# A list-scheduled transformer kernel: order of FFN product groups, a reordered attention step, and another split of the down projection

## The chip, the cores and the metric

The kernel runs on one core of one Trainium2 chip. The metric is the device time of one execution in microseconds (us). A core has a matrix engine (TensorE, PE in the rows; its weight loads are PEld), VectorE (DVE), ScalarE (ACT), GpSimd (POOL) and SyncE (SP), which here issues all DMAs. Each engine works through its own list of instructions in order.

## The reference

All arrays are float32, the width is 1024, the sequence is 1024 tokens. Two layers stand one behind the other, each a mixer and a feed-forward network (FFN) of hidden width 2816, and then a second block.

```
h = layer_norm(x * alpha + mixer(x))              # even: conv + linear recurrence; odd: attention
h = layer_norm(h * alpha + (silu(h @ w_gate) * (h @ w_up)) @ w_down)

# diff attention of 8 heads, two maps of 64 each, causal by chunks of 64
scores = einsum('bhmqd,bhmkd->bhmqk', q, k); p = softmax(where(mask, scores, NEG))
attn = p[:, :, 0] - lam * p[:, :, 1];  o = rms_norm(attn @ v) * (1 - lambda_init);  return o @ w_out

# second block: modulation by ada(cond), mLSTM + Fourier mixing, then relu(h @ w_ff1 + b)**2 @ w_ff2, width 4096
```

## The kernel before, in words

Every large matrix product runs as three matmuls with split operands (`mm3`, L235 to L237: high by high, low by high, high by low). A weight is loaded into a tile `raw`; `split` (L213, L214) makes the high part with a cast on ACT (`wh`, `wd`, `ht`) and the low part with a subtraction on DVE (`wl`, and again `wd`, `ht`). The order in which instructions stand on each engine comes from a list scheduler that takes ready work by program order, so moving a call in the code moves instructions on all engines; the engines then run the lists in order. Waits between engines are by semaphores.

The up and gate product of an FFN, and the first product of the second block's FFN (FF2 below), uses a scheme of seven products for a 2 x 2 block product. `product` issues them: `corner` (B11, into `wx`, copied to `keep`), T2 (`wy`, copied to `u2`), T1 (`wz`, copied to `p5`), T3 on top of `wy`, `corner2` (B21 on `wx`), B22 and T4. One term is 12 matmuls of 128 x 512. The sums of input rows that the scheme needs are made by `xn.sums` (L144 to L155) and `prepare` (L661 on, with L674 to L677 on the weights). Before the first `product`, `start()` issues six corner products, called fronts here (`EARLY` = 1, 1, 2, 2), from within the last stage of the mixer ahead, where `pipe` calls `more`; each front needs one weight's `wh` and `wl`.

The result of the up and gate products goes to DRAM (`hd`), and the down projection reads it back by `tokens` as tiles `ht`. It runs in parts over the hidden width: `PARTS1` for the two FFNs (8, 6, 4, 4 blocks of 128), `PARTS2` for FF2; for each part it walks over 8 tiles of 128 tokens (`down_tile`, matmuls `dn`, added to `xr` on DVE at L898). The letter of a part says in which pool its weights lie. The last part runs in a pipe with the first stages of what follows (norm, transposes, V weights, `pv` and `pi` matmuls). `weights(j)` loads and splits part j. In FF2 the down weights are scaled on DVE by a row `mrow` that a DMA brings (L1248, L1828), and a bias row is added to `xr` on GpSimd. The pool `rp` of `raw` tiles has three buffers. Beside FFN1 the modulation (`ada`) runs as side work: 48 loads of 512 KB, two steps of it at each down tile (`SDN` = 2).

Attention (`mixer_odd`) walks over 64 steps (head, tile of 128 queries). A step issues: `scores` of the step two further on (matmuls `sc`, L1049 and L1050; then on DVE a memset and the maximum at L1058 or L1063, on ACT exp at L1065, on DVE L1069 to L1072), some fills (12 matmuls each, `pq`, `pv` or `pw`, projections of the next head or of the output), `trans` (transposes `pt`, L1083, copied to `at` by ACT, L1085), more fills, and `pv` (matmuls `po`, L1098; then ACT L1102, GpSimd, DVE L1105 and L1106). `sc` has two PSUM buffers of 1024 columns; from tile 4 on a step takes both.

Of the kernel before, what the change touches and what calls it, by code (L numbers as in the profile page):

```python
# [11 lines left out]
F32R = mybir.dt.float32r  # L12
# [15 lines left out]
NF2 = 4096 // P  # L28
NEG = -1.0e30
EARLY, WAHEAD = (1, 1, 2, 2), 2  # L30
PARTS1 = ((8, "x"), (6, "u"), (4, "x"), (4, "u"))
PARTS2 = ((8, "x"), (6, "u"), (8, "x"), (6, "u"), (4, "x"))
L2 = 2
DV = 1
# [29 lines left out]
ME, MO = (0, 1, 2), (1, 0, 2)  # L64
# [96 lines left out]
class Net:  # L161
# [248 lines left out]
    def mixer_even(self, xr, xn, start):  # L410
# [220 lines left out]
        for c in range(NC1, 4):  # L631
            conv(c, 1)
        more = lambda i: start() if i == NTT - 1 else None
        self.pipe(pre + [(0, lambda i: feat(i - 4)), (LE, prod_a), (LE + ME[0], more), (LE + ME[1], more),
                         (LE + ME[2], more), (LE + 1, norm), (LE + 2, feat), (LE + 3, xn.sums), (LE + 3, more)],
                  range(4, 8))

    def mixer_end(self, xr, xn, layer):
# [61 lines left out]
    def product(self, o, x, keep, finish, sum22, early):  # L700

        nc = self.nc
        if not early:
            px = self.corner(o, x, keep)
        py = self.pa("wy")
        self.term(py, o["S2"], x, "T2", True, True)
        nc.vector.tensor_add(py, py, keep)
        u2 = self.tmp("u2")
        nc.scalar.copy(u2, py)
        pz = self.pa("wz")  # L710
        self.term(pz, o["S1"], x, "T1", True, True)
        p5 = self.tmp("p5")
        nc.scalar.copy(p5, pz)
        nc.vector.tensor_add(pz, pz, u2)
        self.term(py, o["S3"], x, "T3", False, True)
        sum22(py, p5)
        if not early:
            self.corner2(o, x, px, finish)
        self.term(pz, o["S4"], x, "B22", False, True)
        finish(0, 1, pz)  # L720
        self.term(py, o["A22"], x, "T4", False, True)
        finish(1, 0, py)

    def run_ffn(self, nf, x, src, nm, done, parts, down_weight, load, add, stages, side=None, add_half=None):
# [20 lines left out]
        def finisher(q, m):  # L745
            def finish(i, h, p):
                f, d = 2 * q + i, dst(q, i, h)
                done(m, f, d, p)
                if m == nm - 1:
                    j = part_of(f)  # L750
                    nc.sync.dma_start(hd[j][f - edges[j], :, half(h)], d)

            def sum22(py, p5):
                if m == 0:
                    c = dst(q, 1, 1)
                else:
                    c = p5
                nc.vector.tensor_add(c, py, p5)
                finish(1, 1, c)

            return finish, sum22
# [4 lines left out]
        def finish_first():  # L766
            o, p, (q, m), finish = begun.pop(0)
            self.corner2(o, x, p, finish)
# [19 lines left out]
        def prep(n):  # L788
            q, m = order[n]
            return self.prepare(src(2 * q, m), src(2 * q + 1, m), first=(q, m) not in started)  # L790

        o = prep(0)
        while begun:
            finish_first()
        for n, (q, m) in enumerate(order):
            nxt = prep(n + 1) if n + 1 < len(order) else None
            finish, sum22 = finisher(q, m)
            self.product(o, x, keep(q, m), finish, sum22, (q, m) in started)
            if m == nm - 1:
                ctx.pop(q)  # L800
            if n % 2:
                kept.pop(n // 2)
            o = nxt
            steps(SD[n % 2])

        def weights(j):
            n, kind = parts[j]
            ws = []
# [9 lines left out]
                ws.append((t[:, e, :], t[:, e + 1, :]))  # L818
            return ws

        def tokens(j, i):
            n, hs = parts[j][0], []
            for a in range(0, n, 4):
                e = min(n, a + 4)
                shape = (P, 2, e - a, P)
                if add_half is None and j == len(parts) - 1:
                    t = self.u("ht", shape, F32R)
                else:
                    t = self.wp.tile(list(shape), F32R, tag="w", name=self.name("ht"))
                raw = t[:, 1].bitcast(F32)  # L830
                nc.sync.dma_start(raw, hd[j][a:e, :, blk(i)].rearrange("f p t -> p f t"))
                self.split(t[:, 0], t[:, 1], raw)
                hs += [(t[:, 0, b, :], t[:, 1, b, :]) for b in range(e - a)]
            return hs

        todo = [(j, i) for j in range(len(parts)) for i in range(NTT)]
        ws, hs = {0: weights(0)}, {}

        def ahead(n):
            if n < len(todo) and todo[n] not in hs:  # L840
# [136 lines left out]
    def mixer_odd(self, x, xr, xn, start):  # L977
# [190 lines left out]
        for n, (hd, i) in enumerate(steps):  # L1168
            if i == 0:
                if hd < 7:  # L1170
                    for _ in fill:
                        pass

                def filler(hd=hd):
                    if hd < 7:
                        yield from qk(hd + 1)
                    if hd < 6:
                        yield from vals(hd // 2 + 1, hd % 2)
                    else:
                        for _ in last:  # L1180
                            yield

                fill = filler()
                left = list(shares[hd])
            if n + LEAD < len(steps):
                if steps[n + LEAD][1] == 0:
                    assert sum(left[:i]) >= 16
                scores(*steps[n + LEAD])
            k = left[i]
            for _ in range((k + 1) // 2):  # L1190
                next(fill, None)
            trans(hd, i)
            for _ in range(k // 2):
                next(fill, None)
            pv(hd, i)
        for _ in last:
# [3 lines left out]
        more = lambda i: start() if i == NTT - 1 else None  # L1200
        sums = lambda i: xn.sums(i) if i >= 4 else None
        self.pipe([(0, lambda i: heads4(i, 4)), (LO + MO[0], more), (LO + 2, feat), (LO + 1, norm), (LO, o_prod),
                   (LO + MO[1], more), (LO + MO[2], more), (LO + 3, sums), (LO + 3, more)])

    def ada(self):
        nc, A = self.nc, self.A
# [119 lines left out]
    def block2_mix(self, x, xr, xn, start):  # L1326
# [480 lines left out]
        def more(i):  # L1807
            if i == NTT - 1:
# [1 line left out]

        stats = lambda i: self.ln_stats(xr[i])
        self.pipe([(3, stats), (4, stats), (1, prep), (3, norm1), (4, norm2), (2, prod)] + [(m, more) for m in MF]
                  + [(LM, feat), (0, moments), (LM + 1, lambda i: xn.sums(i) if i >= 4 else None), (LM + 1, more)])

    def block2_ff(self, x, xr, out):
        nc, A = self.nc, self.A
        st = {}
        cnt = [0] * NTT

        def done(m, f, d, p):  # L1820
            nc.scalar.activation(d, p, AF.Relu, bias=self.c("b_ff1", f))
            nc.vector.tensor_mul(d, d, d)

        def down_weight(f):
            if f == 0:
                st["g2"] = self.mod_row(5)
            r = self.raw(A["w_f2"][f])
            nc.vector.tensor_mul(r, r, st["g2"])  # L1828
            return r

        def load(i):
            if i == 0:
                st["b2"] = self.u("b2")
                r12 = ROWS.index("b_ff2")
                nc.sync.dma_start(st["b2"], A["rows"][r12:r12 + 1, :].to_broadcast([P, D]))
                nc.gpsimd.tensor_mul(st["b2"], st["b2"], st["g2"])
            xr.append(self.u("xr"))
            nc.sync.dma_start(xr[i], self.xs[2][blk(i), :])

        def add(i, p, first, last):  # L1840
            nc.vector.scalar_tensor_tensor(xr[i], xr[i], ALPHA2 if first else 1.0, p, op0=ALU.mult, op1=ALU.add,
                                           accum_out=self.sum_of(xr[i]) if last and S4 else None)
            if cnt[i] == 1:
                nc.gpsimd.tensor_add(xr[i], xr[i], st["b2"])
            cnt[i] += 1

        def add_half(i, p, cs):
            nc.vector.tensor_add(xr[i][:, cs], xr[i][:, cs], p)

        def parts(i):  # L1850
            return [half(0), half(1)] if i in HN else [slice(0, D)]

        def norm_a(i):
            if i == 0:
                st["gb"] = self.gb("ln2_g", "ln2_b")
            self.ln_stats(xr[i])
            t, g = xr[i], st["gb"][0]
            mu, _, sign = self.moments[id(t)]
            for c in parts(i):
                nc.vector.scalar_tensor_tensor(t[:, c], t[:, c], mu, g[:, c], op0=ALU.subtract if sign > 0 else ALU.add,  # L1860
                                               op1=ALU.mult)

        def norm_b(i):
            t, b = xr[i], st["gb"][1]
            rs = self.moments.pop(id(t))[1]
            for c in parts(i):
                nc.vector.scalar_tensor_tensor(t[:, c], t[:, c], rs, b[:, c], op0=ALU.mult, op1=ALU.add)
                nc.sync.dma_start(out[blk(i), c], t[:, c])

        return self.run_ffn(NF2, x, lambda f, m: A["w_f1"][f], 1, done, PARTS2, down_weight, load, add,  # L1870
                            [(FT, norm_b), (1, norm_a)], add_half=add_half)

# [152 lines left out]
```

## Time and profile before

| | |
|---|---|
| median of 3 runs | 3423.69 us (3421.68 to 3425.16) |
| the profiled execution: its own time | 3421.3 us |
| its span, first to last instruction | 3419.5 us |
| mean granted TensorE clock | 0.985 of full |
| busy: PE, DVE, ACT, POOL | 3269.5, 2185.5, 1412.9, 265.6 us |

PE is busy for 96% of the span, so what the order of the lists can change is the rest, and the stretches in which PE is busy at a lower clock. In the rows below a wait is put down to the last releaser that the profile shows.

### The profile page before, as it was taken

The numbers are of one execution on the slowest core, as the hardware profiler recorded it, in microseconds if no ns is written. First come the engines' busy times: TensorE is split into PE (matmuls) and PEld (weight loads), VectorE is DVE, ScalarE is ACT, GpSimd is POOL, SyncE is SP. The second block draws the span as 40 slices with busy tenths as digits, with TensorE's granted clock in tenths as the row PEclk, the third lists the DMA queues.
The fourth block names the chain that finished last, engine by engine and source line by source line (L and its number), as shares of the span: only waits on it lengthen the run. The fifth ranks groups of instructions, "written<-read, shape, count | busy, mean of one in ns | idle before, by whom it ended". The sixth has DMA issues, their size and how long they took to land.

```text
span 3419.5 us, 40944 instructions
## 1 busy us (share of the span) xinstructions
PE 3269.5 (96%) x15588; PEld 2692.5 (79%) x15588; DVE 2185.5 (64%) x3445; ACT 1412.9 (41%) x2422; POOL 265.6 (8%) x458
## 2 busy tenths in 40 slices
PE   8998999999999999989999999999999989999998
PEld 7776788878877878877788878778777878878887
DVE  8997755555357677676765558654446876566635
ACT  4455433332237667655533332224334554432211
POOL 1011000000020111101000000013001300000201
PEclk9999999999999999999999999999999999999999
DMA  3131322235312111141332238721123333344312
GB/s 126 42 112 62 101 91 74 91 128 169 106 62 71 36 50 50 43 149 56 109 107 99 93 120 290 237 74 47 59 84 106 116 117 117 116 161 165 113 51 79
DMA packets 191764, 348.68 MB, mean 102 GB/s; under 512 B 14384, under 2 KB 105936, under 8 KB 191568
## 3 DMA queue, kind: packets, MB, share of 16 engines
q1 hardware_dynamic: 191568, 346.07, 30.6%
q8 instruction: 122, 2.00, 0.2%
q14 instruction: 74, 0.61, 0.1%
HBM read 268.41 MB, written 72.36 MB: 100 GB/s over the span
## 4 chain that ended last, share of the span: by engine, by line
PE 66%; DVE 13%; ACT 9%; DMA 5%; issue 4%; POOL 3%; SPq 0%; POOLq 0%; DVEq 0%; ACTq 0%
PE dn L236 6%; PE dn L235 6%; PE dn L237 6%; PE wy L235 4%; PE wy L236 4%; PE wy L237 4%; PE wx L235 3%; PE wx L237 3%; PE wx L236 3%; PE pi L235 3%; PE pi L236 3%; PE pi L237 2%; PE wz L235 2%; PE wz L237 2%; PE wz L236 2%
## 5 line engine op out<-in xcount | busy, mean ns | idle before, releaser
L213 ACT CAST wh<-raw 128x1024 fp32r<-128x1024 f32 (+1 forms) x275 | 282.7, 1048 | 405.1 <-DVE raw L677 138.1
L214 DVE TENSOR_TENSOR wl<-raw,wh 128x1024 fp32r<-128x1024 f32 (+1 forms) x275 | 334.3, 1233 | 132.1 <-ACT wh L213 128.1
L213 ACT CAST ht<-ht 128x512 fp32r<-128x512 f32 (+1 forms) x168 | 97.2, 580 | 448.0 <-DMA ht<-hd 438.7
L235 PE MATMUL dn<-wd,ht 128*128 128x512 f32 x704 | 274.4, 391 | 3.3 <-ACT wd L213 3.3
L236 PE MATMUL dn<-wd,ht 128*128 128x512 f32 x704 | 274.8, 390 | 1.3 <-DVE wd L214 1.2
L237 PE MATMUL dn<-wd,ht 128*128 128x512 f32 x704 | 274.4, 390 | 0.0
L235 PE MATMUL dn<-wh,ht 128*128 128x512 f32 x512 | 200.9, 392 | 10.8 <-DVE xr L898 6.7
L214 DVE TENSOR_TENSOR ht<-ht 128x512 fp32r<-128x512 f32 (+1 forms) x168 | 112.3, 673 | 153.2 <-ACT ht L213 152.4
L235 PE MATMUL wx<-bh,wh 128*128 128x512 f32 x480 | 192.2, 400 | 10.6 <-ACT keep L693 4.2
L237 PE MATMUL wx<-bh,wl 128*128 128x512 f32 x480 | 190.2, 397 | 11.2 <-DVE wl L214 11.2
L237 PE MATMUL dn<-wh,ht 128*128 128x512 f32 x512 | 200.3, 391 | 0.4 <-DVE ht L214 0.4
L236 PE MATMUL dn<-wl,ht 128*128 128x512 f32 x512 | 200.2, 391 | 0.0
L236 PE MATMUL wx<-bl,wh 128*128 128x512 f32 x480 | 190.3, 396 | 0.0
L235 PE MATMUL pi<-xh,wh 128*128 128x512 f32 x416 | 168.8, 406 | 7.8 <-DVE xl L214 7.8
L486 DVE SCALAR_TENSOR_TENSOR co<-ga,col,co 128x512 f32<-128x512 f32 (+18 forms) x240 | 165.4, 737 | 0.5
L237 PE MATMUL pi<-xh,wl 128*128 128x512 f32 x416 | 165.0, 397 | 0.0
L236 PE MATMUL pi<-xl,wh 128*128 128x512 f32 x416 | 164.9, 396 | 0.0
L235 PEld LDWEIGHTS dn<-wd,ht 128*128 128x128 f32 x704 | 132.3, 188 | 32.0 <-ACT wd L213 4.6
L236 PEld LDWEIGHTS dn<-wd,ht 128*128 128x128 f32 x704 | 132.4, 188 | 30.3 <-DVE wd L214 2.9
L237 PEld LDWEIGHTS dn<-wd,ht 128*128 128x128 f32 x704 | 132.4, 188 | 27.5
L287 POOL TENSOR_SCALAR nm<-sum 128x1 f32<-128x1 f32 x47 | 15.1, 322 | 1562.8 <-DVE xr L898 1323.1
L898 DVE SCALAR_TENSOR_TENSOR xr<-xr,dn 128x1024 f32<-128x1024 f32 x64 | 77.8, 1216 | 85.5 <-PE dn L237 81.3
(458 smaller groups left out, 8446.4 us busy)
## 6 DMA issues: line engine op xcount, KB each, us to landing
raw<-w_gu SPq DMA_DIRECT2D x100, 512.0 KB
hd<-g SPq DMA_DIRECT2D x152, 256.0 KB
raw<-w_f SPq DMA_DIRECT2D x70, 512.0 KB
ht<-hd SPq DMA_DIRECT2D x136, 256.0 KB
raw<-w_ada SPq DMA_DIRECT2D x48, 512.0 KB
raw<-w_dn SPq DMA_DIRECT2D x44, 512.0 KB
raw<-w_in SPq DMA_DIRECT2D x26, 512.0 KB
raw<-w_out SPq DMA_DIRECT2D x24, 512.0 KB
```

Of the source, the lines that this page charges most:

```text
L213: self.nc.scalar.copy(hi, src)
L214: (self.nc.gpsimd if pool else self.nc.vector).tensor_sub(lo, src, hi.bitcast(F32))
L235: mm(out, l[0], r[0], start=first, stop=False, **kw)
L236: mm(out, l[0], r[1], start=False, stop=False, **kw)
L237: mm(out, l[1], r[0], start=False, stop=last, **kw)
L287: (nc.vector if NMV else nc.gpsimd).tensor_scalar(nm, a, -1.0 / D, None, op0=ALU.mult)
L486: nc.vector.scalar_tensor_tensor(co[c][:, a:hi_], ga[c][:, a - s:hi_ - s], self.c("conv_w", 31 * c + 30 - s), co[c][:, a:hi_], op0=ALU.mul ...
L898: nc.vector.scalar_tensor_tensor(xr[i], xr[i], DN_ALPHA if first else 1.0, p, op0=ALU.mult, op1=ALU.add, accum_out=self.sum_of(xr[i]) if l ...
```

## The change

Six edits are made.

- `PARTS1` becomes 8, 4, 4, 6 blocks, and the `ht` tiles of the last part come from the `raw` pool of three buffers and no longer from another pool.
- In `product`, `corner2` (the 12 matmuls of B21) stands ahead of T3 and no longer behind it.
- `weights(0)`, the first part's down weights, is issued ahead of the last `product` and no longer behind it.
- In three stage pipes the last `more` (fronts five and six) stands ahead of `xn.sums` and no longer behind it.
- An attention step issues first fills, `trans`, `scores` of two steps on, second fills, `pv`.
- In FF2 a multiplication and eight additions of the bias row go from GpSimd to DVE.

```
-PARTS1 = ((8, "x"), (6, "u"), (4, "x"), (4, "u"))
+PARTS1 = ((8, "x"), (4, "u"), (4, "x"), (6, "u"))
...
-                         (LE + ME[2], more), (LE + 1, norm), (LE + 2, feat), (LE + 3, xn.sums), (LE + 3, more)],
+                         (LE + ME[2], more), (LE + 1, norm), (LE + 2, feat), (LE + 3, more), (LE + 3, xn.sums)],
...
         nc.vector.tensor_add(pz, pz, u2)
+        if not early:
+            self.corner2(o, x, px, finish)
         self.term(py, o["S3"], x, "T3", False, True)
         sum22(py, p5)
-        if not early:
-            self.corner2(o, x, px, finish)
         self.term(pz, o["S4"], x, "B22", False, True)
...
             finish, sum22 = finisher(q, m)
+            if nxt is None:
+                ws[0] = weights(0)
             self.product(o, x, keep(q, m), finish, sum22, (q, m) in started)
...
-        ws, hs = {0: weights(0)}, {}
+        hs = {}
...
                 if add_half is None and j == len(parts) - 1:
-                    t = self.u("ht", shape, F32R)
+                    t = self.rp.tile(list(shape), F32R, tag="raw", name=self.name("ht"))
...
+            k = left[i]
+            for _ in range((k + 1) // 2):
+                next(fill, None)
+            trans(hd, i)
             if n + LEAD < len(steps):
                 if steps[n + LEAD][1] == 0:
                     assert sum(left[:i]) >= 16
                 scores(*steps[n + LEAD])
-            k = left[i]
-            for _ in range((k + 1) // 2):
-                next(fill, None)
-            trans(hd, i)
             for _ in range(k // 2):
                 next(fill, None)
             pv(hd, i)
...
-                nc.gpsimd.tensor_mul(st["b2"], st["b2"], st["g2"])
+                nc.vector.tensor_mul(st["b2"], st["b2"], st["g2"])
...
-                nc.gpsimd.tensor_add(xr[i], xr[i], st["b2"])
+                nc.vector.tensor_add(xr[i], xr[i], st["b2"])
```

Three places show how the lists move. The first is DVE's list ahead of FFN0's first product, before; the weight's low part of the last front is `wl_2714`, the sums of the last tiles are `ts_2660` and `ts_2661`, their splits `bl` and `bs`, and `w_390_2755` belongs to the first product.

```order
L151 TENSOR_TENSOR ts_2660<-f_2631,ts_2660 128x512
L152 TENSOR_TENSOR ts_2661<-f_2631 128x512
L153 TENSOR_TENSOR ts_2661<-f_2229,ts_2660 128x512
L887 TENSOR_TENSOR g_2619<-g_2619,wx_2593 128x512
L214 TENSOR_TENSOR bl_2448<-ts_2660,bh_2447 128x8x128
L214 TENSOR_TENSOR bs_2453<-ts_2661,bs_2451 128x2x128
L214 TENSOR_TENSOR bs_2454<-ts_2661,bs_2452 128x2x128
L214 TENSOR_TENSOR bs_2461<-ts_2661,bs_2459 128x2x128
L214 TENSOR_TENSOR bs_2462<-ts_2661,bs_2460 128x2x128
L214 TENSOR_TENSOR wl_2714<-raw_2711,wh_2713 128x1024
L214 TENSOR_TENSOR w_390_2755<-raw_2753,w_390_2755 128x512
```

The same place on DVE in the changed kernel, where the last front's low part is `wl_2698` and the last tiles' sums are `ts_2729` and `ts_2730`.

```order
L214 TENSOR_TENSOR wl_2698<-raw_2695,wh_2697 128x1024
L214 TENSOR_TENSOR bs_2352<-f_2631,bs_2350 128x2x128
L214 TENSOR_TENSOR bs_2353<-f_2631,bs_2351 128x2x128
L153 TENSOR_TENSOR ts_2645<-f_2154,ts_2644 128x512
L214 TENSOR_TENSOR bl_2448<-ts_2644,bh_2447 128x8x128
L214 TENSOR_TENSOR bs_2453<-ts_2645,bs_2451 128x2x128
L214 TENSOR_TENSOR bs_2454<-ts_2645,bs_2452 128x2x128
L214 TENSOR_TENSOR bs_2461<-ts_2645,bs_2459 128x2x128
L214 TENSOR_TENSOR bs_2462<-ts_2645,bs_2460 128x2x128
L890 TENSOR_TENSOR g_2619<-g_2619,wx_2593 128x512
L214 TENSOR_TENSOR w_390_2755<-raw_2753,w_390_2755 128x512
L674 TENSOR_TENSOR raw_2753<-raw_2753 128x512
```

The low part now stands ahead of both groups of sums, and the first product's weight work stands ahead of the last group.

The second place is PE's list in attention at the start of a step, before; the matmuls `pv` are fills.

```order
L237 MATMUL pv_8054<-wh_7912,xl_6695 128x256
L1098 MATMUL po_8092<-v_6832,at_8072 128x128 x4
L1098 MATMUL po_8092<-v_6833,at_8078 128x128 x3
L1049 MATMUL sc_8109<-kh_7555,sq_7553 128x256
L1050 MATMUL sc_8109<-kl_7557,sq_7553 128x256
L1049 MATMUL sc_8109<-kh_7556,sq_7554 128x256
L1050 MATMUL sc_8109<-kl_7558,sq_7554 128x256
L235 MATMUL pv_8127<-wh_7906,xh_6694 128x256
```

In the changed kernel PE's list around the scores of such a step reads so.

```order
L237 MATMUL pv_8036<-wh_7906,xl_6619 128x256
L1086 MATMUL pt_8049<-ident,e_7865 128x128 x4
L1086 MATMUL pt_8056<-ident,e_7865 128x128 x3
L1052 MATMUL sc_8063<-kh_7537,sq_7535 128x128
L1053 MATMUL sc_8063<-kl_7539,sq_7535 128x128
L1052 MATMUL sc_8063<-kh_7538,sq_7536 128x128
L1053 MATMUL sc_8063<-kl_7540,sq_7536 128x128
L235 MATMUL pv_8036<-wh_7912,xh_6618 128x256
```

The scores stood right behind `po` of the step before, and now stand behind the first fills and the transposes of their own step.

The third place is SP's list of DMAs at the end of FF2's products, before; `hd_18281` is written with the products' results, `w_f` are weights.

```order
L751 DMA hd_18281<-g_23612 128x512
L751 DMA hd_18281<-g_23629 128x512 x2
L831 DMA ht_23826<-hd_18277 128x4x128
L751 DMA hd_18281<-g_23612 128x512
L751 DMA hd_18281<-g_23721 128x512
L1248 DMA mrow_23772<-modd 128x1024
L751 DMA hd_18281<-g_23738 128x512
L831 DMA ht_23830<-hd_18277 128x4x128
L1835 DMA b_3846_23834<-rows 128x1024
```

The same DMAs of SP in the changed kernel.

```order
L218 DMA raw_23671<-w_f 128x1024
L218 DMA raw_23676<-w_f 128x1024
L834 DMA ht_23818<-hd_18277 128x4x128
L834 DMA ht_23822<-hd_18277 128x4x128
L751 DMA hd_18281<-g_23612 128x512
L1251 DMA mrow_23663<-modd 128x1024
L751 DMA hd_18281<-g_23628 128x512
L751 DMA hd_18281<-g_23612 128x512
L834 DMA ht_23826<-hd_18277 128x4x128
L751 DMA hd_18281<-g_23628 128x512
```

The row `mrow` stood behind five writes of `hd_18281`, and now stands behind one.

## Rows read from the trace of the kernel before

**Rows 1.** The page's busy times: us, share of the span, instructions.

```profile
PE 3269.5 (96%) x15588; PEld 2692.5 (79%) x15588; DVE 2185.5 (64%) x3445; ACT 1412.9 (41%) x2422; POOL 265.6 (8%) x458
```

**Rows 2.** PE's waits: line, who is waited for; us in total, times, longest.

```profile
PE sc L1049 <- ACT e L1065: 20.1, 15, 5.0
PE wx L237 <- DVE wl L214: 11.2, 3, 4.5
...
PE po L1098 <- ACT at L1085: 8.3, 13, 1.6
...
PE pi L235 <- DVE xl L214: 7.8, 1, 7.8
...
PE dn L235 <- DVE xr L898: 6.7, 5, 2.8
PE wy L235 <- ACT u L709: 5.7, 5, 2.1
...
PE dn L235 <- ACT ht L213: 4.1, 1, 4.1
...
PE dn L235 <- ACT wd L213: 3.3, 2, 2.5
```

**Rows 3.** Windows: length, busy us of PE, PEld, DVE, ACT, POOL, PE clock, DMA, GB/s.

```profile
345.00:420.00 75.00, 70.45 (x304) 56.41 (x303) 56.25 (x84) 34.51 (x62) 0.00 (x0) 0.98 0.32 103
970.00:1070.00 100.00, 90.17 (x503) 77.10 (x502) 58.78 (x89) 54.45 (x94) 19.97 (x32) 0.98 0.22 73
1070.00:1440.00 370.00, 348.29 (x2132) 302.75 (x2131) 261.37 (x548) 263.48 (x598) 44.44 (x96) 1.00 0.16 46
1440.00:1500.00 60.00, 50.30 (x243) 40.29 (x242) 48.80 (x86) 44.92 (x85) 7.57 (x12) 0.91 0.46 141
...
2145.00:2200.00 55.00, 52.24 (x225) 42.63 (x224) 37.51 (x58) 10.90 (x16) 0.00 (x0) 0.97 0.80 257
...
2260.00:2360.00 100.00, 87.61 (x480) 75.92 (x478) 57.90 (x87) 51.44 (x102) 26.41 (x58) 0.93 0.18 61
...
3040.00:3075.00 35.00, 30.44 (x123) 23.04 (x122) 25.64 (x25) 12.69 (x16) 2.95 (x1) 0.95 0.67 218
3075.00:3400.00 325.00, 325.00 (x1435) 268.94 (x1434) 166.44 (x168) 67.71 (x100) 30.67 (x23) 1.00 0.32 102
```

**Rows 4.** PE's timeline at FFN0's last front: start, duration, operation, idle before.

```profile
360.90 0.39 PE L236 MATMUL wx<-bl,wh 128*128 128x512 f32 x1
361.13 0.39 PE L237 MATMUL wx<-bh,wl 128*128 128x512 f32 x1
365.34 0.50 PE L237 MATMUL wx<-bh,wl 128*128 128x512 f32 x1 [3.82 <-DVE wl L214]
...
367.39 0.63 PE L237 MATMUL wx<-bh,wl 128*128 128x512 f32 x1
367.82 0.63 PE L235 MATMUL wx<-bh,wh 128*128 128x512 f32 x1
```

**Rows 5.** DVE's timeline in the same stretch.

```profile
362.73 1.42 DVE L214 TENSOR_TENSOR bs<-ts,bs 128x256 fp32r<-128x256 f32 x4
364.07 1.21 DVE L214 TENSOR_TENSOR wl<-raw,wh 128x1024 fp32r<-128x1024 f32 x1
```

**Rows 6.** DVE's timeline in an attention step, behind `po` and the next scores.

```profile
1116.89 0.21 DVE L1105 TENSOR_SCALAR rs<-rs,r 128x1 f32<-128x1 f32 x1 [0.44 <-POOL rs L261]
...
1118.12 1.23 DVE L1063 TENSOR_REDUCE mx<-sc 128x1 f32<-128x1024 f32 x1
```

**Rows 7.** PE's timeline: the `po` of the step before, right ahead of those scores.

```profile
1111.87 1.28 PE L1098 MATMUL po<-v,at 128*128 128x128 f32 x10
```

**Rows 8.** Timeline of SP's queue and of DVE at the start of FF2's down projection.

```profile
3046.32 0.42 SPq L1248 DMA_DIRECT2D mrow<-modd  x1
...
3050.64 3.50 DVE L1828 TENSOR_TENSOR raw<-raw,mrow 128x1024 f32<-128x1024 f32 x3
```

**Rows 9.** The page's list of DMA issues: operation, times, size of one.

```profile
raw<-w_ada SPq DMA_DIRECT2D x48, 512.0 KB
```

More of the change, by code (lines that the diff above doesn't have):

```diff
@@ L790, in prep @@
             return self.prepare(src(2 * q, m), src(2 * q + 1, m), first=(q, m) not in started)
[L792 to L804, printed above, removed]
         def weights(j):
@@ L819, in weights @@
             return ws
+        ws = {}
+        o = prep(0)
+        while begun:
+            finish_first()
+        for n, (q, m) in enumerate(order):
+            nxt = prep(n + 1) if n + 1 < len(order) else None
+            finish, sum22 = finisher(q, m)
+            if nxt is None:
+                ws[0] = weights(0)
+            self.product(o, x, keep(q, m), finish, sum22, (q, m) in started)
+            if m == nm - 1:
+                ctx.pop(q)
+            if n % 2:
+                kept.pop(n // 2)
+            o = nxt
+            steps(SD[n % 2])
         def tokens(j, i):
@@ L1202, in mixer_odd @@
         self.pipe([(0, lambda i: heads4(i, 4)), (LO + MO[0], more), (LO + 2, feat), (LO + 1, norm), (LO, o_prod),
-                   (LO + MO[1], more), (LO + MO[2], more), (LO + 3, sums), (LO + 3, more)])
+                   (LO + MO[1], more), (LO + MO[2], more), (LO + 3, more), (LO + 3, sums)])
     def ada(self):
@@ L1812, in block2_mix @@
         self.pipe([(3, stats), (4, stats), (1, prep), (3, norm1), (4, norm2), (2, prod)] + [(m, more) for m in MF]
-                  + [(LM, feat), (0, moments), (LM + 1, lambda i: xn.sums(i) if i >= 4 else None), (LM + 1, more)])
+                  + [(LM, feat), (0, moments), (LM + 1, more), (LM + 1, lambda i: xn.sums(i) if i >= 4 else None)])
     def block2_ff(self, x, xr, out):
```

## The prediction

> **What bounds the kernel now.** I read the busy times first: PE is busy for 3269.5 us of a span of 3419.5 [rows 1]. DVE and ACT have a third and more of their time free, so no other engine is the bound over the whole span. What an order can win is PE's idle time, 150 us, and the time that PE works at half clock. Next I read the list of PE's waits [rows 2]. The reader is to see that few kinds carry much of it, and that most belong to places which the change touches: the attention scores wait for exp (20.1 us in 15 waits), a front waits for the low part of its weight (11.2 us in 3), `po` waits for the copies of the transposes (8.3 us), the drain of an FFN into the next mixer waits once for 7.8 us, down tiles wait for `xr` (6.7 us), `ht` (4.1 us) and `wd` (3.3 us), and `wy` waits for `u2` (5.7 us). Last I read windows by stage [rows 3], for two things: PE's busy time, and the clock. A mean clock of c over a window of T us costs about (1 - c) x T beside the idle time, since the two levels are 1.2 and 2.4 GHz: at FFN0's last front matmuls start 0.23 us apart, and after a wait of 3.82 us they start 0.43 us apart [rows 4]. So 1.5 us go there in 345 to 420, 5.4 us in 1440 to 1500 and 7 us in 2260 to 2360. In 1070 to 1440, with 21.7 us idle in small pieces, the clock is 1.00: these waits cost only themselves.
>
> **The change part by part.**
>
> *Fronts ahead of the sums.* PE stops at 361.5 and resumes at 365.34, when DVE's `wl` of 1.21 us, begun at 364.07, is done [rows 4, 5]. Ahead of it DVE worked on the sums of the last tiles and their splits (four splits alone 1.42 us [rows 5]). The list of the changed kernel has this `wl` ahead of two groups of sums, so the wait of 3.82 us should go, and the same at FFN1 and FF2 (11.2 us together). But DVE's total work up to the first product is the same, and that product needs the sums and its own low parts. PE would come to it some 4 us earlier, and part of the wait appears there. I take two thirds of the 11.2 us as gained, 7.5, and half of the clock (1.5 us at each of three places, by the window of FFN0), 2. Sum: 9.5 us. Bounds: 0, if all reappears, and 11.2 + 4.5 = 15.7.
>
> *Attention.* No instruction is added. In a step before, `po` starts at 1111.87 and runs 1.28 us [rows 7], and the next scores stand right behind it. DVE's list has the maximum of these scores behind the scaling of `po`'s result, which waits for ACT and GpSimd: that scaling starts at 1116.89 and the maximum only at 1118.12 [rows 6], 5 us after `po` ended. Exp follows, and the scores of the next step, which need both buffers free, wait for it. In the changed order `po` has 12 fills and the transposes behind it before the scores come. The maximum is no earlier, but the next scores are asked for later by these fills and transposes: 12 fills of 512 columns take 12 x 0.23 = 2.8 us, of 256 columns about half, 1.4 us. The waits for exp average 20.1 / 15 = 1.3 us, so most are covered. The copies `at` stand ahead of the next exps on ACT and meet `po` only after the second fills, so the 8.3 us should shrink too. What is late next is exp in the steps with 256-column fills, and the end of the last head: it has no fill after its fifth tile, so the last scores stand behind transposes and `po` with nothing to cover them; I charge 2 us. I take 3/5 of 20.1 + 8.3, 17 us, half of the 5.4 us of clock in 1440 to 1500, 2.7, less 2: 18 us. Bounds: 0, and 28.4 + 5.4 = 33.8.
>
> *FF2's first down weights.* `mrow` is issued at 3046.32, behind writes that wait for products, and the scaling of the weights begins at 3050.64 [rows 8]. In 3040 to 3075 PE idles 4.6 us and the clock costs 1.7 [rows 3]. In SP's new list `mrow` stands behind one of these writes and the weights' loads ahead of them. I take 4.5 us; bounds 0 and 6.3.
>
> *`corner2` earlier, and the first weights in FFN0 and FFN1.* The 12 matmuls now stand between T1 and T3, so `u2` has 2.8 us more. Of the 5.7 us of waits for `u2` [rows 2] two waits of about 2 us are those of the last products, where nothing else covers. Against it, T4's cover behind the sum of T3 falls from 24 matmuls to 12, 2.8 us; and the weights' casts stand ahead of the last product's copies on ACT, which I price at a cast of the size of L213's, about 1 us, at one or two products. I take 1.5 us gained; bounds: a loss of 3 and a gain of 4.
>
> *Parts 8, 4, 4, 6 and `ht` in the `raw` ring.* Three places move. In FFN1's second part 16 steps of `ada` (two at each of 8 tiles) now share 8 x 24 matmuls x 0.23 = 44 us, where six blocks gave 66. They load 16 x 512 KB [rows 9], the next part's weights 4 more, and the `ht` tiles (128 x 4 x 128 floats, 256 KB) 8 x 256 KB: 12.6 MB. At the 257 GB/s of 2145 to 2200 [rows 3] that is 49 us, 5 us too long; before, the same rush cost a wait of 2.8 us and 1.6 us of clock there. Net loss: about 0.5 us. The Trainium skill, "DMA: Bandwidth & Descriptors", section "Specifications", gives a core some 358 GB/s of memory bandwidth; by that figure, an estimate, the 12.6 MB would take 35 us and this place would gain the 4.4 us instead. The trace stays at 257 GB/s with DMA 0.80 busy, so it does not bear the figure out here.
>
> The tails: FFN0's (970 to 1070) idles 9.8 us and loses 2 by clock [rows 3]. With six blocks in the last part each down tile covers 36 matmuls, 8.3 us, rather than 24, 5.5; but `ht` and the V weights now take turns in three buffers, and a weight whose turn comes late holds the `pv` behind it. I take no change, bounds a gain and a loss of 4. FFN1's (2260 to 2360) idles 12.4 us, 7.8 of it the drain and 4.1 one `ht`, and loses 7 by clock. The longer tiles should halve the drain and spare some clock, 3.7 + 2.8 = 6.5, and the ring should give back about 3 at the V weights. The whole part: 6.5 - 3 - 0.5 = 3 us gained. Bounds: a loss of 8 (the 4.1 us wait once more in each tail) and a gain of 15 (three quarters of the 19.4).
>
> *FF2's adds.* Nine DVE instructions more, 1.22 us each by the size of L1828's, 11 us, in a stretch of 325 us where DVE works 166 and PE never stops [rows 3]. Nothing. Without that cover it would be the 11 us.
>
> Sum: 9.5 + 18 + 4.5 + 1.5 + 3 = 36.5. The profiled execution took 3421.3 us, 2.4 less than the median, so 3384.8 on its scale and 3387 on the median's.
>
> **The rivals.**
>
> *The waits in attention only move.* For it: exp needs both buffers' maxima in turn, each 1.23 us [rows 6], and with 256-column fills the next scores come barely 2.3 us later. Against it: the mean wait is 1.3 us. If attention gives 4 instead of 18: 3401.
>
> *More comes back, clock included.* If half of what the bounds allow beyond my sum returns (15.7 + 33.8 + 6.3 + 4 + 15 = 75, less 36.5, halved: 19): 3368. For it: each long wait that goes takes its slow stretch along. Against it: DVE's work per stage is the same.
>
> *The ring turns into the bound: slower.* In both last parts each tile needs two `ht` loads in turn through three buffers, with V weights and the next stage's weights among them, in SP's order. One `ht` that came late cost 4.1 us [rows 2]. If every one of 16 tiles paid it, 66 us: 3390 + 66 = 3456. It decides from (33.5 + 7) / 16 = 2.5 us a tile. Against it: a tile has 8.3 us of matmuls, and DMA is 0.18 to 0.22 busy in the tails.
>
> *Nothing to see.* Gains of a third and a loss of some 10 in the tails: 3420.
>
> **How the numbers follow.** The measurement can tell about 0.2%, 7 us, from no change. Forecast (3376 to 3397) 0.55; waits only move (3397 to 3416) 0.22; more comes back (below 3376) 0.12; same 0.05; slower 0.06. Faster: 0.55 + 0.22 + 0.12 = 0.89, of which 0.01 goes to slower for what I have not seen. The range reaches to 3368, the second rival's price, and to 3412, which leaves out a third of the first rival.
>
> **What the profile will show.** Right: the waits of `wx` for `wl` at the third place of each FFN gone or below 1 us; `sc` for exp below 9 us, `po` below 3; `dn` for `wd` gone; `pi` for `xl` at half; the clock at 1.00 in attention and above 0.95 in FFN1's tail. Wrong: new waits of `wy` or `wx` in the first product, `dn` for `ht` or `pv` for `wh` in the tails, `dn` for `xr` in FFN1's second part. What would make it wrong most is attention, half of the sum: if `sc` still waits, the fills are too short.

## The result and the profile after

The changed kernel takes 3380.25 us (median of 4 runs, 3379.6 to 3383.95), the kernel before 3423.4 in the same comparison; the ratio is 0.9876, 95% interval 0.9859 to 0.9893. The forecast was 3387 with a range of 3368 to 3412. The profiled execution has a span of 3378.2 us, 41.3 less than before, and a mean clock of 0.987.

The sum was right to within 7 us, but not its terms. The list of PE's waits answers [rows 2]; columns as there.

```profile
PE sc L1052 <- ACT e L1068: 8.3, 5, 2.9
...
PE dn L235 <- DVE xr L901: 7.7, 7, 2.4
PE pt L1086 <- ACT v L964: 7.5, 6, 1.4
...
PE pt L1123 <- DMA o<-od: 5.7, 2, 5.0
PE pi L235 <- ACT wh L213: 4.6, 1, 4.6
...
PE wx L235 <- ACT keep L693: 3.8, 3, 1.9
...
PE wy L235 <- ACT wh L213: 3.0, 1, 3.0
...
PE po L1101 <- ACT at L1088: 2.2, 4, 0.7
...
PE wy L235 <- ACT u L709: 2.2, 3, 1.2
...
PE dn L235 <- ACT wd L213: 0.8, 1, 0.8
```

The scores' wait fell from 20.1 to 8.3 us, `wx` for `wl` is gone from the list (11.2), `po` for `at` fell from 8.3 to 2.2, the drain of FFN1 from 7.8 to 4.6, `dn` for `wd` from 3.3 to 0.8. New are the transposes' waits for the copies of `v`, one of 5.0 us for `o` (the longest was 1.5 before), and 3.0 us of `wy` for `wh` at FF2's first product.

The windows of the same stages answer [rows 3]; columns as there.

```profile
340.00:415.00 75.00, 72.17 (x316) 57.87 (x315) 60.75 (x93) 40.33 (x73) 0.00 (x0) 1.00 0.33 110
960.00:1060.00 100.00, 93.97 (x516) 79.82 (x516) 61.32 (x92) 54.88 (x95) 14.32 (x25) 0.98 0.32 111
1060.00:1416.00 356.00, 340.33 (x2135) 301.07 (x2134) 263.41 (x545) 264.14 (x598) 51.61 (x96) 1.00 0.16 48
1416.00:1482.00 66.00, 49.80 (x236) 40.35 (x235) 50.60 (x89) 44.94 (x86) 6.28 (x12) 0.87 0.47 147
2124.00:2170.00 46.00, 43.96 (x193) 35.64 (x192) 38.35 (x56) 8.50 (x12) 0.00 (x0) 1.00 0.84 269
...
2238.00:2338.00 100.00, 94.33 (x557) 83.50 (x556) 57.94 (x92) 56.50 (x113) 35.16 (x55) 0.97 0.31 102
3002.00:3037.00 35.00, 33.63 (x147) 27.13 (x146) 29.35 (x31) 16.60 (x22) 0.00 (x0) 1.00 0.75 249
3035.00:3360.00 325.00, 325.00 (x1436) 269.10 (x1435) 157.20 (x171) 66.50 (x98) 10.70 (x16) 1.00 0.31 100
```

The fourth row is the one to look at: in the last attention heads the clock is now 0.87 (0.91 before) and PE idles 16.2 us of 66. That is the one stage which got clearly worse. The table below places the gain: the start of the first matmul of each stage in one trace less that in the other, and the difference from stage to stage. FFN1's parts, which have other sizes now, are set against each other by the count of matmuls done. Each entry comes from one trace of each kernel; how far a stage moves by itself is told with e9 and e12.

| stage | after less before, us | forecast |
|---|---|---|
| ahead of FFN0's fronts | +1.0 | 0 |
| fronts, FFN0, FFN1, FF2 | -5.9, -6.3, -2.2 | -9.5 |
| products between first and last | -0.8, -0.3, -1.5 | 0 |
| last products of FFN0, FFN1 | -0.9, -2.3 | -1.5 |
| start of FF2's down projection | -5.6 | -4.5 |
| FFN0's tail | -3.4 | 0 |
| FFN1's second and third parts | +0.8 | +0.5 |
| FFN1's tail and drain | -9.0 | -3.5 |
| attention, heads 0 to 5 | -14.6 | -18 for all heads |
| attention, heads 6 and 7, and its end | +7.9, +1.6 | (in the row above) |
| from FFN1's drain to FF2's fronts | -1.1 | 0 |
| rest of FF2's down projection, end | 0, +1.3 | 0 |

### The profile page after: what moved, and what is told of

Its sections match the earlier page's. It is cut to its first block, busy times and chain, and to the rows that moved or that the text cites. A ratio compares the mean times of both kernels' runs of the same rounds, so it can differ in the third digit from the quotient of the medians.

```text
span 3378.2 us, 40985 instructions
## 1 busy us (share of the span) xinstructions
PE 3247.2 (96%) x15588; PEld 2687.4 (80%) x15588; DVE 2183.4 (65%) x3454; ACT 1415.6 (42%) x2422; POOL 251.5 (7%) x449
## 5 line engine op out<-in xcount | busy, mean ns | idle before, releaser
L235 PE MATMUL wx<-bh,wh 128*128 128x512 f32 x480 | 189.8, 395 | 10.2 <-ACT keep L693 3.8
L235 PEld LDWEIGHTS dn<-wh,ht 128*128 128x128 f32 x512 | 96.5, 188 | 28.5 <-issue 3.7
```

The source lines that it names most:

```text
L235: mm(out, l[0], r[0], start=first, stop=False, **kw)
```

## The experiments

In all diffs the base is the kernel named. A run's median is set against that of the kernel before on the same chip; these vary from 3419 to 3427 us, so the ratio counts. It is not quite the quotient of the two medians: a gain in us worked out from it can lie up to 4 us from the difference of the medians.

**e1, the fronts alone**, on the kernel before (the end of one line in one of three pipes shown):

```
-    ... (LE + 3, xn.sums), (LE + 3, more)],
+    ... (LE + 3, more), (LE + 3, xn.sums)],
```

> The kernel before with one edit alone: in the three stage pipes the last fronts stand ahead of the sums. Theory (the gains add up place by place, as the two traces show them): 5.9 us at FFN0, 4.9 at FFN1 and 3.9 at FF2, 14.6 together, so about 3409, and nothing in attention. Rival (earlier fronts ask for their weights earlier, and these loads are what delays the o tiles in the last attention heads): the same gains, but some 8 us lost between the sixth head and the end of attention, about 3417.

Measured 3410.37 us, 0.9956 (0.9942 to 0.997). By the trace the three places gave 5.9, 6.3 and 2.4 us, 14.6. From the start of head 6's `po` to the end of attention it is 1.4 us faster than before, where the rival had 8 us lost: the rival falls. At the places the gains are those of the changed kernel; the span is only 7.4 us shorter in this trace, which is the slowest of e1's runs, so some 7 us of them were lost again elsewhere, 3.2 of these in FFN0's products and 2.4 over the whole of attention.

**e2, the attention order alone**, on the kernel before (the last attention hunk of the change).

```
-            if n + LEAD < len(steps):
...
-                scores(*steps[n + LEAD])
             k = left[i]
...
             trans(hd, i)
+            if n + LEAD < len(steps):
...
+                scores(*steps[n + LEAD])
```

> The kernel before with the attention step's new order alone. Theory (the new order itself delays the o tiles behind six weight loads in the last two heads): 14 to 15 us gained in heads 0 to 5, some 8 lost in heads 6 and 7, 5 to 7 in sum, about 3417, with a wait of about 5 us of the output transposes for o. Rival (the loss belongs to the fronts, not to the new order): the whole 14 to 20 us stays, about 3406, and no such wait.

Measured 3414.69 us, 0.9979 (0.997 to 0.9988), 7 us. In the trace, 14.7 us are gained from the first scores to the start of head 6's `po` and 8.1 are lost from there to the end of attention. The waits of that end, columns as above:

```profile
PE sc L1049 <- ACT e L1065: 7.9, 4, 2.9
PE pt L1120 <- DMA o<-od: 4.6, 2, 3.7
PE pw L235 <- ACT y L1123: 2.9, 1, 2.9
...
```

The loss belongs to the new order and comes without the fronts' edit.

**e3, parts and ring alone**, on the kernel before.

```
-PARTS1 = ((8, "x"), (6, "u"), (4, "x"), (4, "u"))
+PARTS1 = ((8, "x"), (4, "u"), (4, "x"), (6, "u"))
...
-                    t = self.u("ht", shape, F32R)
+                    t = self.rp.tile(list(shape), F32R, tag="raw", name=self.name("ht"))
```

> The kernel before with parts 8, 4, 4, 6 and the last part's ht tiles in the raw ring alone. Theory (places add up): 3.4 us gained in FFN0's tail and 8.2 from FFN1's second part to its drain, 11.6 in sum, about 3412. Rival (part of these gains came from the first weights and the earlier corner2, which end the products earlier): 3 to 6 us, about 3419.

Measured 3412.15 us, 0.9966 (0.9954 to 0.9979), 11.6 us by the ratio. In the trace, whose span is 7.3 us shorter, the tails gained 3.2 (FFN0) and 9.0 (FFN1), and the second and third parts lost 5.0; the rest is spread. The theory holds for the tails: their gains need none of the other edits.

**e4, the new order in heads 0 to 5 only**, on the changed kernel.

```
+            if hd >= 6:
+                if n + LEAD < len(steps):
...
+                    scores(*steps[n + LEAD])
             k = left[i]
...
             trans(hd, i)
-            if n + LEAD < len(steps):
...
-                scores(*steps[n + LEAD])
+            if hd < 6:
+                if n + LEAD < len(steps):
...
+                    scores(*steps[n + LEAD])
```

> The changed kernel with one difference: heads 6 and 7 keep the old order of the attention step (scores first). Theory (only the last two heads lose by the new order): the o tiles stand behind three weight loads as before, the 5 us wait for o goes, and of the 8 us lost there most come back: 3371 to 3376 against 3380. Rival (the old order's own waits there, 5.0 us for exp, 1.6 us for the copies and their half clock, return in their place): 3380, within 2.

Measured 3368.49 us, 0.9844 (0.9831 to 0.9858), below the changed kernel's 0.9876, and better than I had expected. From head 6 to the end of attention it is 1.0 us faster than before, where the changed kernel is 7.9 slower. The old waits did return, 5.0 us for exp, 4.1 for the copies and 2.9 for `o`, but in sum they cost less than the new ones.

**e5, corner2 and the first weights alone**, on the kernel before.

```
         nc.vector.tensor_add(pz, pz, u2)
+        if not early:
+            self.corner2(o, x, px, finish)
         self.term(py, o["S3"], x, "T3", False, True)
         sum22(py, p5)
-        if not early:
-            self.corner2(o, x, px, finish)
...
+            if nxt is None:
+                ws[0] = weights(0)
             self.product(o, x, keep(q, m), finish, sum22, (q, m) in started)
...
-        ws, hs = {0: weights(0)}, {}
+        hs = {}
```

> The kernel before with two edits alone: corner2 ahead of T3, and the first down weights issued ahead of the last product. Theory (the gains stand where the two traces differ): about 2 us at the last product of FFN0, 2 to 4 at that of FFN1, 5.6 at the start of FF2's down projection (half of it clock); 9 to 11 in sum, about 3411. Rival (only the row mrow that comes earlier matters, and the other products give back what they win): 5 to 6 us, about 3416.

Measured 3407.67 us, 0.9969 (0.9958 to 0.998), 10.6 us by the ratio, as the theory had it. The stages: 4.2 in FFN0's products, 3.6 in FFN1's, 4.7 at the start of FF2's down projection.

**e6 and e7, e4 with the old parts**, once with the old pool for `ht` (e6, both hunks) and once with the ring (e7, the first hunk alone).

```
-PARTS1 = ((8, "x"), (4, "u"), (4, "x"), (6, "u"))
+PARTS1 = ((8, "x"), (6, "u"), (4, "x"), (4, "u"))
...
-                    t = self.rp.tile(list(shape), F32R, tag="raw", name=self.name("ht"))
+                    t = self.u("ht", shape, F32R)
```

> The kernel of e4 with the old parts 8, 6, 4, 4 and the last part's ht in the old pool. Theory (the new parts are worth in company what they were worth alone, 8 to 12 us): 3377 to 3380. Rival (earlier weights and the new order have taken away the waits that the parts removed): within 3 us of e4's 3368.5.

> The kernel of e4 with the old parts 8, 6, 4, 4, but the last part's ht tiles in the raw ring. Theory (what helps the drain of FFN1 is six blocks in the last part, and the ring alone is at best neutral): as e6, 3377 to 3382. Rival (the ring, which leaves buffers of the old pool free for the next stage, is what helps): as e4, 3367 to 3371.

Measured 3380.4 us, 0.9887 (0.9867 to 0.9907), and 3383.22, 0.9899 (0.9882 to 0.9917), against e4's 0.9844. So parts and ring together are worth 0.43% in company too (e6 against e4), and the ring without the parts shows no gain (e7 against e6). FFN1's tail shows where. PE's waits there, e7 first:

```profile
PE pi L235 <- DVE xl L214: 8.0, 1, 8.0
PE pv L235 <- ACT xh L213: 6.2, 1, 6.2
...
```

In the changed kernel, with the ring and six blocks in the last part:

```profile
PE pi L235 <- ACT wh L213: 4.6, 1, 4.6
PE pv L236 <- DVE wl L214: 0.8, 2, 0.7
...
```

In the middle of the tail a down tile waits 4.1 us for `ht` in e6, as in [rows 2]; with the ring alone a `pv` waits 6.2 us in its place (e7); with the longer tiles and the ring neither is left, and the drain is shorter by 3 us. Six blocks with `ht` in the old pool were not run, so whether the ring is needed for them stays open.

**e8, the o tiles in a buffer of their own**, on the changed kernel.

```
-            o = self.u("o", (P, H512))
+            o = self.mp.tile([P, H512], F32, tag="o512", name=self.name("o"), bufs=1)
```

> The changed kernel with one difference: the o tiles of the attention output lie in one buffer of their own and no longer in the big shared pool; the step order is the changed one for all heads. The third load of o then stands ahead of the six weight loads. Theory (the loss in the last two heads is that queue, for more than half): the wait of 5.0 us for o goes, with its 6.8 us at half clock, 3372 to 3375. Rival (the new order itself is too dry there, or the wait goes over to the next load behind the weights): 3378 to 3381.

Measured 3367.79 us, 0.9852 (0.9835 to 0.9869). That is better than I had expected; its interval still meets the changed kernel's (0.9859 to 0.9893), so the gain over it rests on the stages of the two traces, read below. The queue which the buffer goes round is seen on SP's timeline of the changed kernel in the last heads:

```profile
1452.54 0.58 SPq L1120 DMA_DIRECT2D o<-od  x1
1454.08 14.97 SPq L218 DMA_DIRECT2D raw<-w_gu  x6
1469.14 0.38 SPq L1136 DMA_DIRECT2D xr<-spill  x1
1469.58 0.42 SPq L1120 DMA_DIRECT2D o<-od  x1
```

Before, three such loads stood there:

```profile
1480.92 5.88 SPq L218 DMA_DIRECT2D raw<-w_gu  x3
1486.85 0.43 SPq L1133 DMA_DIRECT2D xr<-spill  x1
1487.37 0.38 SPq L1117 DMA_DIRECT2D o<-od  x1
```

SP works through its list in order. Six loads of FFN1's first weights now stand ahead of the third `o`, and each waits until DVE is done with one of three `raw` buffers. SP's own waits from 1452 to 1471 us:

```profile
SPq L218 <- DVE wl L214: 8.6, 3, 4.3
SPq L218 <- DVE wol L214: 4.9, 3, 2.2
```

So 15 us pass before SP comes to `o`. PE meets it 7 us later:

```profile
1476.88 1.11 PE L1123 MATMUL pt<-ident,o 128*128 128x128 f32 x4 [4.97 <-DMA o<-od]
```

In e8 no wait of PE's matmuls for `o` is left; the longest that are left in these heads:

```profile
PE sc L1052 <- ACT e L1068: 5.0, 2, 2.5
PE pt L1086 <- DVE y L1127: 2.0, 1, 2.0
PE pt L1086 <- DVE e L1075: 1.5, 1, 1.5
...
```

The rival falls: from head 6 to the end of attention e8 is 4.5 us faster than before, 12.4 better than the changed kernel, and the clock is at its lower level there for 3.4 us rather than for 17.1.

**e9, fewer loads in FFN1's second part**, on e8.

```
-                steps(SDN)
+                steps(1 if j == 1 else SDN)
```

> The kernel of e8 with one step of ada instead of two at each down tile of FFN1's second part; the steps left over run in the third part, so nothing is left out. Theory (in the second part of four blocks the loads come too slowly, so that DVE adds late: the waits of dn for xr, 2 us in each of parts two and three): they go in part two and stay or grow in part three, so the time moves by less than 4 us either way, 3364 to 3370. Rival (the waits are DVE's own order and not the loads): the waits of part two stay as they are.

Measured 3370.22 us, 0.9841 (0.9824 to 0.9857), no different from e8 by their intervals. PE's waits in FFN1's second part (2108 to 2153 us) and behind it in the third (to 2200), for e8:

```profile
PE dn L235 <- DVE xr L901: 2.3, 4, 1.5
...
PE dn L235 <- DVE xr L901: 1.7, 2, 1.5
```

The same two windows in e9:

```profile
PE dn L235 <- DVE xr L901: 0.5, 1, 0.5
...
PE dn L235 <- DVE xr L901: 3.3, 4, 1.2
```

In these two traces the waits move with the steps: part two ends 3.0 us earlier than in e8, and part three gives 1.9 of it back. One trace of each does not settle it, since the two parts together moved by -3.7 to +3.5 us against the kernel before in kernels that leave them as they were (e1, e12). That DVE adds late because a load comes late is not shown by itself, since a step of `ada` is a load and DVE's work on it.

**e10, e4 and e8 together.** 

> The changed kernel with both: heads 6 and 7 in the old step order, and the o tiles in their own buffer. Theory (both took away the same thing, the wait for o behind the weight loads): no better than e8 alone, 3365 to 3370, with the old order's wait of 5 us for exp. Rival (two separate losses): 3356 to 3360.

Measured 3365.11 us, 0.9824 (0.9809 to 0.9838). By the ratios it lies some 10 us below e8, with intervals that meet; by the traces its span is 3365.7 and e8's 3362.4 (e10's slowest run and e8's fastest). In heads 6 and 7 it is 7.2 us faster than before, e8 4.5. So the old order seems to gain a little there, and which of the four versions (e4, e8, e9, e10) is the fastest stays open. All four ratios lie below the changed kernel's 0.9876; only e8's interval meets its.

**e11 and e12, the own buffer in the kernel before**, alone and with the new order.

> The kernel before, with the o tiles in a buffer of their own as in e8 and nothing else. Theory (in the old order only three loads stand before the third o, and PE waits little for it: 1.3 us and 1.5 us): at most 3 us gained, 3420 to 3424. Rival (the buffer is worth its 12 us whatever the order of the step): about 3411.

> The kernel before with the attention step's new order and the o tiles in a buffer of their own. Theory (the new order is worth 14 to 15 us in heads 0 to 5 and some 5 more in heads 6 and 7 once o is not late): 18 to 21 us, 3402 to 3405. Rival (heads 6 and 7 gain nothing): 14 to 15 us, about 3409.

Measured 3411.7 us, 0.9972 (0.9962 to 0.9982), and 3408.85, 0.9956 (0.994 to 0.9971). Here both of my expectations fell, and the rivals came out. The buffer gains 10 us in the old order as well, where the profile had shown but three short waits for `o`, 2.8 us; and buffer and new order together gave 15 us by the ratio (13 by the medians), with nothing gained in heads 6 and 7. From the start of head 6's `po` to the end of attention, against the kernel before:

| | `o` in the shared pool | `o` in its own buffer |
|---|---|---|
| scores first | 0 (before), -1.0 (e4) | -6.9 (e11), -7.2 (e10) |
| scores behind the transposes | +7.9 (after), +8.1 (e2) | -4.5 (e8), -0.5 (e12) |

In three kernels that leave attention and the pool as they were (e1, e3, e5) this stage moved by -0.9 to -1.5 us, so differences of that size tell nothing. Two things cost time in the last heads, and each makes the other dearer: the new order costs 3 to 6 us with the own buffer and 8 to 9 in the shared pool; the shared pool costs 6 to 7 in the old order and 9 to 12 in the new one.

How the shared pool holds the loads back is seen in the issues of all `o` (the starts of the first and of the last stand at the end), for the kernel before, e11, the changed kernel and e8:

```profile
L1117 SPq DMA_DIRECT2D o<-od x16: 319/382/1084, 1461.6 to 1597.0; - x16
L1117 SPq DMA_DIRECT2D o<-od x16: 319/320/372, 1323.5 to 1589.7; - x16
L1120 SPq DMA_DIRECT2D o<-od x16: 319/384/1228, 1437.1 to 1581.9; - x16
L1120 SPq DMA_DIRECT2D o<-od x16: 319/320/373, 1300.8 to 1565.2; - x16
```

With its own buffer the first `o` is issued some 140 us earlier, in either order. The new buffer also leaves the shared pool one kind of tile less to hold; a larger shared pool was not run, so how much of the gain is due to that stays open.

## Why the prediction was right, and where it failed

*Attention* was the step that failed: 18 us forecast, 5.1 by the stages, 7 alone (e2). In heads 0 to 5 the direction was right. The scores' wait for exp fell from 15.1 us to 0.4 there and `po`'s from 4.0 to 1.1, and 14.6 us were gained (14.6 to 14.8 in every kernel with the new order there). Only 6.0 of them are idle time, since new waits of the transposes took the place of a part, six of up to 1.4 us for `v`'s copy and six of up to 1.3 us for the rope on DVE:

```profile
PE pt L1086 <- ACT v L964: 7.5, 6, 1.4
PE pt L1086 <- DVE t L1011: 4.2, 6, 1.3
```

The rest is busy time, which the prediction did not count: it had these waits cost only themselves (see the last section).

In heads 6 and 7 I had charged 2 us for the end without fills and credited 3/5 of their waits (5.0 us for exp, 4.3 for the copies) and half of the clock. Instead the stage lost 7.9. Two causes, by the table above: the order itself (the scores still wait 2.5 and 2.9 us for exp; that the fills are too short to cover it is my reading) and SP's queue, which I followed at FF2's start but not at this place. The stall lies on a load that the edit does not name: the scheduler put six weight loads ahead of it where three had stood. The shared pool is part of the cause: with a buffer of its own (e8) the third `o` is issued at 1448.45 us, ahead of the first of the six loads at 1454.75.

*Fronts* were right in kind and too small: 14.4 us rather than 9.5, near the upper bound of 15.7. The term that was too small is the clock: I took 1.5 us at each place by FFN0's window, but the windows at FFN1 and FF2 have 0.94 and 0.91, which is 3.6 and 5.4 us. Before:

```profile
1640.00:1700.00 60.00, 55.95 (x232) 44.73 (x230) 44.22 (x67) 28.21 (x49) 0.00 (x0) 0.94 0.31 107
2740.00:2800.00 60.00, 51.24 (x206) 40.60 (x207) 46.24 (x75) 32.85 (x60) 1.51 (x2) 0.91 0.35 110
```

The same stretches after:

```profile
1625.00:1685.00 60.00, 58.59 (x251) 46.43 (x251) 46.92 (x70) 29.54 (x51) 0.00 (x0) 1.00 0.37 122
2707.00:2767.00 60.00, 51.87 (x214) 40.91 (x215) 48.16 (x77) 33.73 (x62) 1.50 (x2) 0.94 0.37 119
```

At FFN0 and FFN1 the waits (3.82 and 2.9 us) and the clock came back in full, since the first product, whose work on DVE now stands earlier too, waited for less than 1 us in all at each. At FF2 2.2 us came of a wait of 4.5 and the clock: there the wait did reappear, 3.0 us of `wy` for `wh`.

*FF2's first down weights*: 4.5 forecast, 5.6 measured. `mrow` is issued at 2990.0, 25 us ahead of the first down matmul at 3014.7, where it had been 8:

```profile
L1251 SPq DMA_DIRECT2D mrow<-modd x2: 384/404/424, 2598.4 to 2990.0; - x2
```

*corner2*: 1.5 forecast; the last products gave 3.2, and e5 has 10.6 us in all for this and the weights against 6. The waits for `u2` fell from 5.7 to 2.2 us; no wait that T4's shorter cover would bring is in the list.

*Parts and ring*: 3 forecast, 11.6 in stages (3.4 + 9.0 - 0.8), 11.6 alone. The second and third parts came out near the forecast (+0.8 against +0.5), which says little: the same stretch lost 5.0 in e3, and it moves by some 3.5 us either way without the edit. Under-sized were the tails. I had the ring cost 3 us at FFN1's V weights, and 0.8 was paid; the `ht` wait of 4.1 us went with the longer tiles, and I had left it standing; FFN0's tail, where I took nothing, gained 3.4, and there the wait of 4.3 us of `pv` for `xh` is gone.

*The adds on DVE* were not run alone; the stretch has PE at 325.00 of 325 us as before, so no gain or loss could come of them there.

The slower rival, the ring as the bound, did not show: `dn` for `ht` is 0.2 us in FFN1's tail. On the DMA rate: the second part ran at 269 GB/s with the DMA engines 0.84 busy, a little above the 257 that I used, and the stretch just ahead of it, 2060.3 to 2147.3 in the trace before, had run at 281. So 257 was no limit; by 281, an estimate, the 12.6 MB take 45 us and not 49. The Trainium skill's 358 GB/s ("DMA: Bandwidth & Descriptors", "Specifications") was reached in none of the windows shown. My sum came out because the tails and fronts gave some 14 us more than forecast and attention 13 less. The forecast total is thus right partly by luck.

Of the signs that I had named, the scores' 8.3 us, `po`'s 2.2 and FFN1's tail at 0.97 came out; the clock of 1.00 in attention did so in heads 0 to 5 alone, and of the wrong signs a new wait of `wy` in the first product came at FF2. One reading of the range was off: above 3412 lies a fifth of the first rival's span (3397 to 3416), not a third.

## What to carry to other kernels

When a list scheduler decides, an edit of one loop can also move the loads that stand in the same queue: follow the DMA issuer's list at the place where the loop runs out of work, not only the engines' lists. Here a small load whose tile shares a pool with others was issued late and then stood behind big ones; a buffer of its own of 2 KB a partition was worth 6 to 7 us in that stage in the old order and 9 to 12 in the new one. Longer last tiles before a drain, with their inputs in another pool, were worth 0.43% here; the other pool by itself showed no gain.

## What the runs showed that I had not expected

Waits in a profile do not hold all of a stage's loss. In heads 0 to 5 PE's idle time fell by 6.0 us (21.7 in 370, 15.7 in 356 us), but PE's busy time fell too, from 348.29 to 340.33 us for as many matmuls (2132 and 2135), of which a stretch of half clock, 3.4 us long, explains some 1.7. The same windows with the instructions on the scores `sc` alone, before and after (behind a window and its length stands PE's busy time):

```profile
1070.00:1440.00 370.00, 72.35 (x298) 49.96 (x298) 79.62 (x150) 79.78 (x204) 0.00 (x0) 1.00 0.16 46
1060.00:1416.00 356.00, 66.74 (x298) 48.72 (x298) 80.26 (x150) 80.26 (x204) 0.00 (x0) 1.00 0.16 48
```

The same for `po`:

```profile
1070.00:1440.00 370.00, 58.04 (x432) 53.45 (x432) 16.69 (x48) 22.18 (x96) 1.00 0.16 46
1060.00:1416.00 356.00, 56.12 (x432) 53.95 (x433) 16.72 (x48) 22.16 (x96) 1.00 0.16 48
```

So the same 298 matmuls of the scores are busy for 5.6 us less, and the 432 of `po` for 1.9: just the kinds whose waits went. (Matmuls overlap, so such numbers do not add up to PE's.) That they count as busy while they start late is my reading of it. In e11's last heads it is otherwise: of the 6.9 us gained there the idle time holds 4.9 (13.4 before, 8.5 in e11; the waits for `o` were 2.8 of it), and a shorter stretch of half clock, 6.8 us rather than 10.2, explains 1.7 more.

The clock held 1.00 over the 356 us with 15.7 us of idle time in pieces of up to 1.4 us, and in the 66 us behind it, with 16.2 us in pieces of up to 5.0, it fell to 0.87.
